# adaLN vectors made on TensorE, and native fp32 for the first sixteen products of both up products, in a diffusion block on one core

## The chip, the cores and the metric

The kernel runs on one core of one Trainium2 chip. The metric is the device time of one execution in microseconds. A core has TensorE (matrix products into PSUM), VectorE, ScalarE, GpSimd, and queues that issue DMAs; here SyncE's queue (SP) issues almost all loads and stores.

## The reference

A block of a diffusion model: 1024 latent tokens `x` of width 1024, 256 context tokens `ctx`, two conditioning vectors `c` (for the latent tokens) and `c_ctx` (for the context).

```python
def adaln(cond, w, b):                      # w: 1024 x 9216
    m = jax.nn.silu(cond) @ w + b
    return [t[..., None, :] for t in jnp.split(m, N_MOD, axis=-1)]   # nine vectors of 1024

def half_step_ffn(x, mods, g_pre, g_post, w_gu, w_down):
    shift, scale, gate = mods
    h = modulate(rms_norm(x, g_pre), shift, scale)
    g, u = jnp.split(h @ w_gu, 2, axis=-1)                           # the up product, 2 x 2816 wide
    y = (jax.nn.silu(g) * u) @ w_down                                # the down product
    return x + 0.5 * gate * rms_norm(y, g_post)
```

Vectors 0, 1 and 2 are shift, scale and gate of the first FFN, 3, 4 and 5 those of the middle part (a gated short convolution beside an S5 scan, joined by an output projection), 6, 7 and 8 those of the second FFN. Latent and context tokens go through the first FFN and into the S5 scan; behind it only the latent tokens go on. All inputs are fp32.

## The kernel before

**Products and operands.** A product of two fp32 matrices is made from operands that are split in two parts of the type fp32r: ScalarE copies the high part, VectorE subtracts it from the source (`split`, line 157; `wop` for weights, 591; `hop` for activations, 494). Three fp32r products then stand for one: high x high, high x low, low x high.

**The latent up product** (`g_lat`, 596) is a Strassen-like scheme: for each of 22 column blocks `f` of 128 gate and 128 up columns there are seven products `m` = 1 to 7 instead of eight, each over four k-tiles of 128 and 512 columns, so 4 x 3 matmuls of 128x512. 22 x 7 = 154 products form one FFN. `seq` is their order by hand: first sixteen early ones (`order1`, `order2`: m = 1 for f = 0 to 3, then m = 2, 5 and 3 likewise), then the rest. `prep` (656) forms the weight operand of one product from raw weight tiles (for m = 1 and 2 a half of one tile, for m = 5 a sum, for m = 3 three operations), with sums on VectorE, and splits it; `prod` (687) issues the matmuls and the evacuation from PSUM; `prepare` (756) runs `prep` up to four products ahead. Raw weights stand in four tiles `wr` of 512 KB; `fetch` (646) may load a tile anew when the last product that needs the old content has been prepared (`loads[...][2] < done`). `hops` (499) forms the seven activation operands in the order m = 1, 2, 5, 3, 7, 6, 4, the later ones in place over the earlier (`self.sub(b11, b12, b11)` for m = 5), and keeps the split ones in `hb`.

**The start.** `run` (1629) loads four blocks of `x`, then the columns of vectors 1 and 0 of adaLN in two halves of 512 columns, then four more blocks of `x`. Strings written by hand give the order in which the pieces are issued: `S0` loads, `S1` the hops (`h`), the normalization of the second blocks (`q`), the second half of adaLN (`a`), weight fetches (`f`), preparations (`w`) and products (`p`, `P`). VectorE keeps the order of the program in this part (`G0`); elsewhere a planner orders the instructions of each engine.

**adaLN before.** For each row tile of 128 of `w_ada`, VectorE multiplies a 128x1024 tile by the column of silu(c) in `scol` and adds to an accumulator (`ada_acc`, 280); eight tiles give one vector for one condition. `ada_col` (287) turns the accumulator by a 32x32 transpose and a reduction on VectorE and one small product on TensorE. For vectors 0 and 1 of the latent tokens the sum over partitions is made by `first_sum` (380) with a column of ones.

**Fillers.** Work that may lie anywhere in a stage is a generator, and `self.step()` (122) advances it: in the first FFN after 34 empty steps (`FW`) vectors 1 and 0 for the context, then 2, 3 and 4 for both conditions, then `s5_params` (1088), three steps (`FN`) at each product with m = 3, 4 or 6, so nine per seven products; before the last products the filler is run to its end and the normalization of the context follows (`side`, 1761). In the down stage vectors 5 and 6 are the filler (`fill56`, 1798), in the S5 stage vector 7 (1860), in the second FFN vector 8 (`fill3`, 2011). `ada_mods` (332) loads each 512 KB tile of `w_ada` two steps ahead into a ring of five tiles `tb`, which the early products also use for their results.

**Lines in the profile.** All instructions are issued through one helper, `Lane.call`, so nearly all rows have line 51; rows are told apart by their tiles: `z` large operands and hops, `w` split weights, `wr` raw weights, `t` temporaries, `tb` the ring, `scol` silu of the conditions, `ps` PSUM, `red` and `mod` the adaLN columns, `sd` the stored result of the up product.

Of the kernel before, what the change touches and what calls it, by code (L numbers as in the profile page):

```python
# [13 lines left out]
OP = mybir.AluOpType  # L14
AX = mybir.AxisListType

P = 128
# [51 lines left out]
class Kernel:  # L69
# [111 lines left out]
    def setup(self):  # L181
# [41 lines left out]
        nc.vector.tensor_copy(self.scol, pt[:, :16])  # L223
        self.ones = self.t(cp, [P, 1], "ones")
# [130 lines left out]

    def first_loads(self, side):

        self.mt = self.t(self.cp, [P, 2, KT], "mt")
        for mod in range(2):
            self.modc[mod, 0] = self.mt[:, mod, :]  # L360
# [26 lines left out]
    def first_cols(self, half, pt):  # L387
        sl = slice(4 * half, 4 * half + 4)
        b2 = self.cols[:, 0:16].rearrange("p (m k) -> p m k", m=2)
        self.add(self.mt[:, :, sl], pt[:, :8].rearrange("p (m k) -> p m k", m=2), b2[:, :, sl])  # L390
        self.stt(self.mt[:, 1, sl], self.mt[:, 1, sl], 1.0, self.gpre(0)[:, sl], OP.add, OP.mult)
# [107 lines left out]
    def hops(self, stages, blocks, hb):  # L499
# [4 lines left out]
        for src, m in stages:  # L504
# [8 lines left out]
            for k in range(4):  # L513
# [82 lines left out]
    def g_lat(self, wgu, hb, sd, fills, early, late, held):  # L596
# [59 lines left out]
        def prep(f, m):  # L656
# [26 lines left out]
            wops[f, m] = self.wop(x)  # L683
# [3 lines left out]
        def prod(f, m):  # L687
# [7 lines left out]
            for k in range(4):  # L695
                wh, wl = w[:, 0, k * P : (k + 1) * P], w[:, 1, k * P : (k + 1) * P]
# [57 lines left out]
        look, done = 4, 0  # L754

        def prepare(n, eager=True):
            nonlocal done
            while done < min(n, len(seq)):
                fetch(done)
                prep(*seq[done])  # L760
# [4 lines left out]
        def step(n):  # L765
            prod(*seq[n])

# [12 lines left out]
        for n in range(next(count), len(seq)):  # L780
# [4 lines left out]
            if seq[n][1] in (3, 4, 6):  # L785
                self.step(fills)
# [1320 lines left out]
```

## Time and profile before

| what | value |
|---|---|
| median of 3 runs | 2108.68 us (2104.74 to 2113.64) |
| the profiled execution's own time | 2107.51 us |
| its span (first to last instruction) | 2105.7 us |
| TensorE, busy time | 1937.8 us, 9018 matmuls |
| VectorE, busy time | 1586.3 us, 2727 instructions |
| ScalarE, busy time | 838.5 us, 1482 instructions |
| GpSimd, busy time | 199.7 us, 106 instructions |
| DMA | 368.30 MB, mean 175 GB/s |

Times in the profile run from the span's start. Busy is the time in which an engine has an instruction under way; matmuls are pipelined, so a busy TensorE is not always at its peak. The clock column is TensorE's granted clock as a share of full speed, the DMA column the busy share of the core's 16 DMA engines. The stages in order: start and up product of the first FFN to about 556, up product of the context to about 723, the down products to about 1000, the projections, S5 and convolution to about 1250, output projection to about 1403, second FFN's up product to about 1885, its down product to the end.

### The profile page before, as it was taken

How to read it: one execution, taken by the hardware profiler on the slowest of the kernel's cores; microseconds unless marked ns; L12 is line 12 of the kernel's file. 1: busy time of each engine (PE TensorE's matmuls, PEld its weight loads, DVE VectorE, ACT ScalarE, POOL GpSimd, SP SyncE). 2: the span in 40 equal slices, each digit the busy share in tenths (PEclk: the TensorE clock that was granted, in tenths of full speed). 3: DMA queues.
4: the chain of work that ended last, by engine and by line, in shares of the span. 5: the costliest groups of instructions: out<-in, count | busy, mean ns of one | idle time of the engine just before them, and what ended most of it. 6: DMA issues, size and time to landing. Idle time of an engine off the chain costs nothing.

```text
span 2105.7 us, 25356 instructions
## 1 busy us (share of the span) xinstructions
PE 1937.8 (92%) x9018; PEld 1592.4 (76%) x9018; DVE 1586.3 (75%) x2727; ACT 838.5 (40%) x1482; POOL 199.7 (9%) x106
## 2 busy tenths in 40 slices
PE   5879989898898979999999899997999999999997
PEld 4568876686798867877887787775788888887775
DVE  6689998998865678798637986488865555576977
ACT  5433323243343334466532334354333333334543
POOL 0000000042336200000002430010000000000000
PEclk9889999999999989999999999998999999999999
DMA  8347453255578989367587543143642222277554
GB/s 299 93 146 253 141 177 113 86 146 169 170 224 240 343 303 303 117 239 257 173 234 222 189 141 110 40 151 97 202 150 80 84 86 81 84 252 267 192 189 152
DMA packets 342604, 368.30 MB, mean 175 GB/s; under 512 B 47376, under 2 KB 254924, under 8 KB 342476
## 3 DMA queue, kind: packets, MB, share of 16 engines
q1 hardware_dynamic: 340172, 358.28, 53.3%
q10 hardware_dynamic: 2304, 8.39, 1.0%
q8 instruction: 71, 1.16, 0.2%
q14 instruction: 57, 0.47, 0.1%
HBM read 294.50 MB, written 74.17 MB: 175 GB/s over the span
## 4 chain that ended last, share of the span: by engine, by line
PE 61%; DVE 21%; DMA 9%; issue 4%; ACT 2%; POOL 1%; SPq 1%; DVEq 0%; ACTq 0%; POOLq 0%
PE ps L51 61%; DVE t L51 7%; DVE z L51 6%; DVE w L51 4%; DVE tb L51 3%; DMA wr<-in_ffn_w_gu 2%; DMA tb<-in_w_ada 2%; DMA wr<-in_ffn_w_down 1%; SPq L51 1%; POOL tb L51 1%; DMA z<-in_w_ada 1%; ACT w L51 1%; DMA z<-sd 1%; ACT t L51 1%; ACT z L51 1%
## 5 line engine op out<-in xcount | busy, mean ns | idle before, releaser
L51 PE MATMUL ps<-z,w 128*128 128x512 f32 (+1 forms) x5712 | 1262.3, 382 | 83.1 <-ACT w L51 38.2
L51 PEld LDWEIGHTS ps<-z,w 128*128 128x128 f32 x5712 | 1019.7, 194 | 304.4 <-ACT w L51 44.8
L51 PE MATMUL ps<-w,w 128*128 128x512 f32 x1848 | 434.5, 396 | 19.5 <-DVE w L51 14.1
L51 PEld LDWEIGHTS ps<-w,w 128*128 128x128 f32 x1848 | 350.3, 191 | 101.2 <-DVE w L51 20.2
L51 ACT ACTIVATE w<-wr 128x512 fp32r<-128x512 f32 (+1 forms) x286 | 215.8, 758 | 360.1 <-PE ps L51 280.2
L51 DVE TENSOR_TENSOR w<-wr,w 128x512 fp32r<-128x512 f32 (+1 forms) x280 | 253.4, 909 | 94.4 <-ACT w L51 88.5
L51 ACT ACTIVATE w<-t 128x512 fp32r<-128x512 f32 x308 | 186.9, 626 | 270.5 <-DVE t L51 181.8
L51 DVE TENSOR_TENSOR w<-t,w 128x512 fp32r<-128x512 f32 x308 | 212.8, 701 | 61.5 <-ACT w L51 61.2
L51 DVE TENSOR_TENSOR t<-t,ps 128x512 f32<-128x512 f32 x150 | 102.5, 685 | 66.5 <-PE ps L51 65.7
L51 ACT ACTIVATE w<-z 128x512 fp32r<-128x512 f32 x110 | 69.2, 630 | 148.3 <-PE ps L51 142.2
L51 DVE TENSOR_TENSOR t<-wr 128x512 f32<-128x512 f32 x148 | 101.1, 695 | 30.9 <-DMA wr<-in_ffn_w_down 15.0
L51 ACT ACTIVATE t<-ps 128x512 f32<-128x512 f32 (+2 forms) x135 | 73.7, 548 | 118.3 <-PE ps L51 116.8
L51 DVE TENSOR_TENSOR z<-z,z 128x512 fp32r<-128x512 f32 (+3 forms) x127 | 102.1, 839 | 13.9 <-DMA z<-z 7.1
L51 DVE SCALAR_TENSOR_TENSOR tb<-tb,scol 128x1024 f32<-128x1024 f32 x77 | 98.1, 1283 | 6.9 <-DMA tb<-in_w_ada 6.7
L51 DVE TENSOR_TENSOR w<-z,w 128x512 fp32r<-128x512 f32 x110 | 76.0, 691 | 30.2 <-ACT w L51 30.0
L51 ACT ACTIVATE t<-z 128x1024 bf16<-128x1024 f32 (+3 forms) x132 | 75.4, 605 | 44.7 <-DVE z L51 31.4
L51 ACT ACTIVATE t<-t 128x512 f32<-128x512 f32 (+1 forms) x83 | 51.9, 625 | 103.2 <-DVE t L51 102.7
L51 POOL TENSOR_TENSOR z<-z,z 128x1024 f32<-128x1024 f32 x24 | 84.7, 3552 | 80.0 <-PE ps L51 44.3
L51 PE MATMUL ps<-z,t 128*128 128x512 f32 x384 | 89.9, 395 | 1.1 <-ACT t L51 1.1
L51 PEld LDWEIGHTS ps<-z,t 128*128 128x128 f32 x384 | 72.1, 188 | 18.4 <-ACT t L51 1.5
L51 POOL TENSOR_TENSOR tb<-tb 128x512 f32<-128x512 f32 x24 | 35.8, 1506 | 456.1 <-DVE t L51 434.9
L51 DVE TENSOR_TENSOR z<-t,ps 128x512 f32<-128x512 f32 (+1 forms) x52 | 29.6, 570 | 53.3 <-PE ps L51 52.6
(124 smaller groups left out, 1391.0 us busy)
## 6 DMA issues: line engine op xcount, KB each, us to landing
wr<-in_ffn_w_gu SPq DMA_DIRECT2D x156, 512.0 KB, 4.4
wr<-in_ffn_w_down SPq DMA_DIRECT2D x198, 256.0 KB, 4.5
tb<-in_w_ada SPq DMA_DIRECT2D x64, 512.0 KB, 4.5
sd<-z SPq DMA_DIRECT2D x44, 512.0 KB, 4.7
z<-sd SPq DMA_DIRECT2D x88, 256.0 KB, 5.4
z<-in_w_ada SPq DMA_DIRECT2D x24, 512.0 KB, 6.0
wr<-in_ffn_w_down SPq DMA_DIRECT2D x22, 512.0 KB, 4.5
wr<-in_w_in SPq DMA_DIRECT2D x20, 512.0 KB, 4.6
```

Source lines behind the costliest of these rows:

```text
L51: r = f(*a, **kw)
```

## The change

adaLN is computed on TensorE for all vectors but 8. `srep` holds each column of silu(c) and silu(c_ctx) alternately 32 columns wide; with it as the 128x32 stationary operand, a product with 256 columns of `w_ada` gives both conditions at once in 32 partitions of PSUM, and four such products go to the four groups of 32 partitions (columns of the array). All operands are plain fp32. For vectors 0 and 1 this stands at the start (`first_mm`), for both conditions. Vectors 2 to 7 are one filler of the first FFN (`ada_pe`): four loads in the first four of seven steps, then sixteen products in one burst, two bursts a vector, then a copy, two transposes and two additions. The fillers of the down stage and the S5 stage fall away. TensorE keeps the program's order in the start and in the whole up product of the first FFN. The filler advances twelve steps per seven products, after 22 empty ones.

In both up products the sixteen early products take plain fp32 operands: the weight operand isn't split, and `hr` keeps the unsplit activation. A raw weight tile used by the early products with m = 1 or 2 is loaded anew only when those products have been issued (`free`). The split activations are still made, for the other 18 blocks.

```diff
 def setup
+        self.srep = self.t(cp, [P, KT, 32], "srep")
+        nc.scalar.activation(
+            self.srep.rearrange("p k (n c) -> p n c k", c=2),
+            pt[:, :16].rearrange("p (c k) -> p c k", c=2).unsqueeze(1).to_broadcast([P, 16, 2, KT]), AF.Copy,
+        )
...
+    def ada_pe(self, plan, gap):
+        nc = self.nc
+        seq = [(n, b) for n in range(len(plan)) for b in range(2)]
+        after = iter(())
+
+        def cols(pt, mod, done):
+            rows = self.t2([P, 256])
+            nc.scalar.activation(rows, pt[:, :256], AF.Copy)
+            yield
+            pt = self.ps()
+            for b in range(2):
+                self.tr(pt[:, b * P : b * P + P], rows[:, b * P : b * P + P], P)
+            for cond in range(2):
...
+                col = self.t(self.cp, [P, KT], f"mod{mod}_{cond}")
+                self.add(
+                    col.rearrange("p (j b) -> p j b", b=2),
+                    pt[:, : 2 * P].rearrange("p (b j r) -> p j b r", b=2, j=4)[:, :, :, cond],
+                    self.b_ada(mod).rearrange("p (j b) -> p j b", b=2),
+                )
+                self.modc[mod, cond] = col
+            yield
+            if done:
+                yield from done() or ()
+
+        for n, b in seq:
+            ws = []
+            for g in range(gap):
+                if g < 4:
+                    ws.append(self.ada_load(plan[n][0], 4 * b + g, self.ta()))
+                next(after, None)
+                yield
+            if b == 0:
+                pt = self.ps()
+            for k, w in enumerate(ws):
+                for j in range(4):
+                    nc.tensor.matmul(
+                        pt[32 * j : 32 * j + 32, :256], self.srep[:, 4 * b + k, :], w[:, 256 * j : 256 * j + 256],
+                        start=b == 0 and k == 0, stop=b == 1 and k == 3,
+                    )
+            self.td_(*ws)
...
-    def first_acc(self, mod, acc):
-        for kt in range(KT):
-            self.ada_acc(acc, self.ws[mod, kt // 2][:, kt % 2, :], kt, 0)
-            yield
-
-    def first_sum(self, mod, acc, pt):
-        for k in range(4):
-            c = 4 * mod + k
+    def first_mm(self, pt, mod, kt, w):
+
+        for h in range(2):
+            j = 32 * (2 * mod + h)
             self.nc.tensor.matmul(
-                pt[:, c : c + 1], acc[:, k * P : (k + 1) * P], self.ones, start=True, stop=True
+                pt[j : j + 32, :256], self.srep[:, kt, :], w[:, 256 * h : 256 * h + 256], start=kt == 0, stop=kt == KT - 1
             )
...
 def hops
+                if m in hr:
+                    hr[m].append(c)
...
 def g_lat
+        nraw = sum(m in (1, 2) for _, m in early)
+
+        def free():
+            return min(done, sent) if sent < nraw else done
 
         def fetch(n, most=len(loads)):
-            while most and at[0] < len(loads) and (n is None or loads[at[0]][3] <= n) and loads[at[0]][2] < done:
+            while most and at[0] < len(loads) and (n is None or loads[at[0]][3] <= n) and loads[at[0]][2] < free():
...
-            wops[f, m] = self.wop(x)
+            wops[f, m] = x if (f, m) in early else self.wop(x)
...
             for k in range(4):
+                if (f, m) in early:
+                    nc.tensor.matmul(pt, w[:, k * P : (k + 1) * P], hr[m][k], start=first and k == 0, stop=k == 3, **on)
+                    continue
...
-            if seq[n][1] in (3, 4, 6):
-                self.step(fills)
+            self.step(fills[seq[n][1] - 1])
             step(n)
...
 def run
+        for mod in (1, 0):
+            for kt in range(KT):
+                self.first_mm(pt, mod, kt, self.ws[mod, kt // 2][:, kt % 2, :])
+        self.scale(xt, self.rsq(ss), nc.scalar)
...
 def accs2
             for kt in range(KT):
-                self.ada_acc(acc, self.ws[kt], kt, 0)
-                yield
-            for mod in range(2):
-                self.first_sum(mod, acc[:, mod, :], pt)
+                for mod in range(2):
+                    self.first_mm(pt, mod, kt, self.ws[kt][:, mod, :])
...
 def fill
-            yield from self.ada_mods([
-                (1, (1,), lambda: self.ada_scale(1, 1, 0)),
-                (0, (1,), None),
-                (2, (1, 0), gates1),
-                (3, (1, 0), None),
-                (4, (1, 0), scales4),
-            ])
+            yield from self.ada_pe([
+                (2, gates1),
+                (3, None),
+                (4, scales4),
+                (5, lambda: self.ada_gate(5, 0, 1, False, 2)),
+                (6, None),
+                (7, lambda: self.ada_scale(7, 0, 2)),
+            ], GAP)
             yield from self.s5_params()
...
+        self.nc.order(True, "tensor")
         for _ in ffn:
             pass
+        self.nc.order(False, "tensor")
...
-        def fill56():
-            for _ in range(DW):
-                yield
-            yield from self.ada_mods([
-                (5, (0,), lambda: self.ada_gate(5, 0, 1, False, 2)),
-                (6, (0,), None),
-            ])
-
-        self.fill = fill56()
...
-        self.fill = self.ada_mods([(7, (0,), lambda: self.ada_scale(7, 0, 2))], 1)
...
-S1 = 'wahhaahaahafPpaaqwhafpahpwhwhhwqqqqqqqqqqqqpqqqqPeePhhhPhhhhehPhhpewwhhhPPPphPwhhehPh'
+S1 = 'whhhhfPpaqwhafphpwhwhhwqqqqqqqqqqqqpqqqqPeePhhhPhhhhehPhhpewwhhhPPPphPwhhehPh'
...
-DW = 0
-FW = 34
-FN = 3
+FW = 22
+FN = (2, 2, 1, 1, 2, 2, 2)
+GAP = 7
...
-G0 = ('vector',)
+G0 = ('vector', 'tensor')
```

## Rows read from the trace of the kernel before

**Rows 1.** The page's first part: busy us (share of the span) xinstructions.
```profile
PE 1937.8 (92%) x9018; PEld 1592.4 (76%) x9018; DVE 1586.3 (75%) x2727; ACT 838.5 (40%) x1482; POOL 199.7 (9%) x106
```

**Rows 2.** Windows: stretch, length, busy us by engine, clock, DMA share, GB/s.
```profile
28.00:116.80 88.80, 66.07 (x256) 49.58 (x256) 62.44 (x101) 42.09 (x71) 0.00 (x0) 0.85 0.44 138
116.80:356.70 239.90, 226.69 (x942) 180.37 (x942) 223.19 (x334) 78.36 (x136) 0.00 (x0) 0.96 0.56 175
356.70:500.00 143.30, 134.07 (x564) 106.98 (x564) 126.53 (x315) 48.54 (x83) 35.76 (x24) 0.98 0.41 117
500.00:556.00 56.00, 52.31 (x255) 42.55 (x254) 47.14 (x83) 25.14 (x45) 2.89 (x3) 0.97 0.63 200
723.00:768.00 45.00, 34.04 (x140) 26.15 (x138) 44.69 (x66) 16.01 (x28) 0.00 (x0) 0.91 1.04 393
1060.00:1112.00 52.00, 49.70 (x268) 42.26 (x267) 22.32 (x23) 17.84 (x33) 2.73 (x1) 1.00 0.88 223
1403.20:1483.20 80.00, 60.47 (x257) 46.05 (x255) 65.72 (x114) 43.21 (x75) 2.41 (x1) 0.87 0.41 125
1483.20:1885.00 401.80, 400.04 (x1724) 324.47 (x1724) 244.16 (x378) 140.08 (x241) 0.00 (x0) 1.00 0.37 120
```

**Rows 3.** Lines by form, TensorE, windows 2, 3, 4, 4, 5 and 8 above.
```profile
L51 PE MATMUL ps<-z,w 128*128 128x512 f32 x924 | 226.5, 406 | 17.1 <-ACT z L51 9.9 <-ACT w L51 3.2 <-DVE tb L51 2.4
...
L51 PE MATMUL ps<-z,w 128*128 128x512 f32 x561 | 134.3, 400 | 9.2 <-ACT w L51 7.3 <-DVE t L51 1.8
...
L51 PE MATMUL ps<-z,w 128*128 128x512 f32 x174 | 43.9, 408 | 3.1 <-ACT w L51 2.5 <-DVE t L51 0.4 <-ACT t L51 0.2
L51 PE MATMUL ps<-z,w 128*128 128x256 f32 x65 | 8.2, 282 | 0.0
...
L51 PE MATMUL ps<-w,w 128*128 128x512 f32 x132 | 33.4, 410 | 2.6 <-DVE w L51 1.9 <-ACT w L51 0.6
...
L51 PE MATMUL ps<-z,w 128*128 128x512 f32 x1657 | 386.3, 395 | 1.8 <-DVE w L51 1.6 <-ACT w L51 0.2
```

**Rows 4.** Lines by form, VectorE, 116.8 to 356.7: the adaLN groups.
```profile
L51 DVE SCALAR_TENSOR_TENSOR tb<-tb,scol 128x1024 f32<-128x1024 f32 x56 | 71.1, 1283 | 4.6 <-DMA tb<-in_w_ada 4.5
...
L51 DVE STREAM_TRANSPOSE tb<-tb 128x1024 f32<-128x1024 f32 x8 | 10.0, 1245 | 0.0
L51 DVE TENSOR_REDUCE red<-tb 128x32 f32<-128x1024 f32 x8 | 9.7, 1218 | 0.0
```

**Rows 5.** Lines by form, TensorE, whole run: a native fp32 product's instructions.
```profile
L51 PE MATMUL ps<-tb,z 128*128 128x160 f32 x128 | 21.0, 311 | 2.1 <-DMA z<-pd 2.1
```

**Rows 6.** Timeline of TensorE in the S5 stage: start, length, form, count.
```profile
1121.84 2.78 PE L51 MATMUL ps<-tb,z 128*128 128x160 f32 x20
...
1163.47 1.05 PE L51 MATMUL ps<-t,z 128*128 128x128 f32 x8
```

**Rows 7.** Timeline of all engines, 84 to 92: early products with m = 3.
```profile
84.56 0.63 ACT L51 ACTIVATE w<-t 128x512 fp32r<-128x512 f32 x1 [8.56 <-DVE t L51]
85.22 0.69 DVE L51 TENSOR_TENSOR w<-t,w 128x512 fp32r<-128x512 f32 x1 [0.69 <-ACT w L51]
85.24 3.31 PE L51 MATMUL ps<-z,w 128*128 128x512 f32 x12 [2.18 <-ACT w L51]
...
89.85 0.69 DVE L51 TENSOR_TENSOR t<-t,wr 128x512 f32<-128x512 f32 x1 [3.33 <-DMA wr<-in_ffn_w_gu]
...
91.98 5.49 PE L51 MATMUL ps<-z,w 128*128 128x512 f32 x12 [3.42 <-ACT w L51]
```

**Rows 8.** The page's DMA issues: KB each, us to landing.
```profile
wr<-in_ffn_w_gu SPq DMA_DIRECT2D x156, 512.0 KB, 4.4
```

**Rows 9.** Waits from 723 to 768: us in total, times, longest.
```profile
ACT w L51 <- DMA wr<-in_ffn_w_down: 18.7, 9, 4.2
...
PE ps L51 <- DVE red L51: 8.4, 1, 8.4
```

**Rows 10.** Lines by form, VectorE, 1060 to 1112: vector 7.
```profile
L51 DVE SCALAR_TENSOR_TENSOR z<-z,scol,z 128x1024 f32<-128x1024 f32 x7 | 11.1, 1589 | 14.3 <-DMA z<-in_w_ada 14.3
```

More of the change, by code (lines that the diff above doesn't have):

```diff
@@ L354, in ada_mods @@
                 yield
+    def ada_pe(self, plan, gap):
[10 more added lines that the diff above has]
+            for cond in range(2):
+                if (mod, cond) in self.modc:
+                    continue
[25 more added lines that the diff above has]
+            self.td_(*ws)
+            if b == 1:
+                for _ in after:
+                    pass
+                after = cols(pt, *plan[n])
+        yield from after
     def first_loads(self, side):
-        self.mt = self.t(self.cp, [P, 2, KT], "mt")
+        self.mts = [self.t(self.cp, [P, 2, KT], f"mt{cond}") for cond in range(2)]
         for mod in range(2):
-            self.modc[mod, 0] = self.mt[:, mod, :]
+            for cond in range(2):
+                self.modc[mod, cond] = self.mts[cond][:, mod, :]
         self.ws = {}
@@ L373, in first_loads @@
             yield
[L375 to L382 removed]
+    def first_mm(self, pt, mod, kt, w):
+        for h in range(2):
+            j = 32 * (2 * mod + h)
             self.nc.tensor.matmul(
[L384 removed]
+                pt[j : j + 32, :256], self.srep[:, kt, :], w[:, 256 * h : 256 * h + 256], start=kt == 0, stop=kt == KT - 1
             )
     def first_cols(self, half, pt):
[L388 to L391 removed]
+        nc = self.nc
+        rows = self.t2([P, 256])
+        nc.scalar.activation(rows, pt[:, :256], AF.Copy)
+        pt = self.ps()
+        for b in range(2):
+            self.tr(pt[:, b * P : b * P + P], rows[:, b * P : b * P + P], P)
+        sl = slice(4 * half, 4 * half + 4)
+        b2 = self.cols[:, 0:16].rearrange("p (m k) -> p m k", m=2)[:, :, sl].rearrange("p m (h b) -> p m h b", b=2)
+        rt = pt[:, :256].rearrange("p (b m h r) -> p m h b r", b=2, m=2, h=2)
+        for cond in range(2):
+            m = self.mts[cond][:, :, sl]
+            self.add(m.rearrange("p m (h b) -> p m h b", b=2), rt[:, :, :, :, cond], b2)
+            self.stt(m[:, 1], m[:, 1], 1.0, self.gpre(0)[:, sl], OP.add, OP.mult)
     def rsq(self, ss):
@@ L497, in hop, with hops @@
         return o
-    def hops(self, stages, blocks, hb):
+    def hops(self, stages, blocks, hb, hr):
         t = [[], []]
@@ L594, in wop, with g_lat @@
         return o
-    def g_lat(self, wgu, hb, sd, fills, early, late, held):
+    def g_lat(self, wgu, hb, hr, sd, fills, early, late, held):
         nc = self.nc
@@ L759, in prepare @@
                 fetch(done)
+                if any((seq[done][0], side) not in raws for side in A[seq[done][1]]):
+                    break
                 prep(*seq[done])
@@ L765, in step @@
         def step(n):
+            nonlocal sent
             prod(*seq[n])
+            sent = n + 1
+            if n < nraw:
+                fetch(None)
         count = itertools.count()
@@ L1641, in run @@
         hb = {m: [] for m in range(1, 8)}
+        hr = {m: [] for m in (1, 2, 5, 3)}
         xt = [self.z() for _ in range(4)]
@@ L1726, in run @@
         hs = [k for k, c in enumerate(S1) if c == "h"]
-        assert S1[: hs[5]].count("a") == 10 and S1[: hs[9]].count("q") == 17
+        assert S1[: hs[5]].count("a") == 2 and S1[: hs[9]].count("q") == 17
         act.update(h=lambda: next(h), q=lambda: next(q), a=lambda: next(a))
@@ L1936, in run @@
         hb = {m: [] for m in range(1, 8)}
+        hr = {m: [] for m in (1, 2, 5, 3)}
         def spl(g):
```

32 lines of the change are left out of this document (7 added, 25 removed).

## The prediction

> **What bounds it now.** The page's first part comes first: TensorE is busy for 92% of the span [rows 1]. A share over the whole run doesn't say where time is lost, so next the windows, cut where the work changes [rows 2], and beside them the count of matmuls in each stretch [rows 3]. The latent up product of the second FFN (1483 to 1885) is the yardstick: 1657 matmuls of 128x512 cover 386.3 us, 0.233 us each, TensorE never waits and the clock is granted in full. Holding the other stretches against 0.233 us shows what each loses. The first FFN from 116.8 to 356.7: 924 x 0.233 = 215.4 us and 3 us of small products, of 239.9: 21 lost. VectorE is busy for 223 of those 240 us; its largest group is the adaLN accumulation, 56 operations of 1283 ns, and with 8 transposes and 8 reductions adaLN takes 91 us of it [rows 4]. From 356.7 to 500 (the S5 parameters): 561 x 0.233 = 130.8 of 143.3, 12 lost. From 500 to 556: 174 x 0.233 + 65 half-width ones at 0.126 + 2 = 50.8 of 56, 5 lost. The start of each up product loses most in proportion: 28 to 116.8 holds the sixteen early products, 192 x 0.233 = 44.8 us of products in 88.8; 1403 to 1483 holds the same in 80. The start of the down stage, 723 to 768, is bounded otherwise: 132 x 0.233 = 30.8 in 45 us, with DMA at 1.04 of its engines and VectorE busy for 44.7. The reader is to see: TensorE sets the time, and what is lost sits where VectorE or DMA is full.
>
> **The change, part by part.** *adaLN leaves VectorE in the first FFN.* Gone are 91 us of VectorE work between 116.8 and 356.7. What it costs now is only the 21 us that TensorE loses there; I take 19 back, bounds 8 and 21, since evacuations and operand splits stay on VectorE (132 us over 240) and can delay a product at times.
>
> *adaLN arrives on TensorE.* Six vectors (2 to 7) x 8 row tiles x 4 products = 192 native fp32 products, each with a 128x32 stationary and 256 columns. In the trace a native product is two instructions: the S5 stage's 64 products of 160 columns are 128 of them, of 311 ns each [rows 5], and twenty of them take 2.78 us [rows 6], so they follow each other by (2.78 - 0.31)/19 = 130 ns; for 128 columns it is about (1.05 - 0.3)/7 = 107 ns. That is 0.83 ns a column in each instruction. So 256 columns cost 2 x 213 = 427 ns, and all of them one behind the other 192 x 0.427 = 82 us: the upper bound. All of it lies on the path, for TensorE has no gap there that lasts. The four products of a row tile go to four different quarters of the array's columns. If four run beside each other, the bound below is 82/4 = 20.5 us. The two instructions of one product share a quarter; if starts keep the program's order, only the second of one and the first of the next run together, which gives 41 us. No row of before shows products on part of the columns, so I take 29 us, between four at once and pairs, and keep 20.5 and 82 for the range. The twelve bursts' edges, the transposes that turn the rows into columns (12 of 128x128 at 0.1) and their copies: +3 us, bounds 1 and 8.
>
> The Trainium skill, "TensorE: Matmul & The Clock Gate", section "Measured speedup vs the span model", gives 2.38x for three column tiles; the same share of four would make the 82 us an estimated 26. Against the change speaks "TensorEngine Tiling (Array Packing)", section "Key Properties": changing the tiling mode drains the engine, so 12 bursts drain it 24 times; the page has no price, and no run here shows one.
>
> *The S5 parameters follow.* Their filling steps come 12 per seven products instead of 9, so the same VectorE work falls on fewer products. Nothing taken off the 17 us lost between 356.7 and 556; bounds 12 lost more and 12 gained. A burst on TensorE also lets VectorE catch up.
>
> *The two vectors at the outset.* Eight accumulations of full and sixteen of half width leave VectorE; both conditions are now made at once, which also drops sixteen loads of 512 KB later. In their place TensorE gets 32 native products per half in program order. Two early products precede those of the second half and the rest stand behind them, so TensorE waits there until the last w_ada tile lands. I count nothing for this alone, nor for the one copy on ScalarE that spreads the conditioning columns: their cover is the DMA of the start, for which before waits too; without it the second half's 32 products are 14 us serial, inside the bounds that follow.
>
> *Native fp32 for sixteen products.* Removed per product: a ScalarE copy of 0.63 us, a VectorE subtraction of 0.69 and the hand-overs between them, 16 times in each FFN; TensorE's start on them is the pattern in [rows 7], where sum, copy and matmul follow each other and then VectorE waits 3.33 us for the next weight tile. Added: a product is 4 x 2 x 0.427 = 3.41 us instead of 12 x 0.233 = 2.80, +0.62, or +10 us of TensorE work per FFN, in stretches that hold 44.8 us of products in 88.8 and 80. And a weight tile is freed only when its product has run, not when it was split: the loads of the next weights (4.4 us to land, [rows 8]) start up to three products later for the second four. From 82 us on, each early product still waits for a load and three VectorE operations, 6.7 us a product as before [rows 7], less the split (1.3 us). A new wait: the subtractions that form the later operands overwrite tiles that native products still read, and splits and evacuations queue behind them on VectorE; the products concerned stand a whole group of four earlier, which is the cover. First FFN: four products' splits and the VectorE time freed, -8, bounds -14 and +5. Second FFN: -5, bounds -12 and +8. If the cover were gone, each would be +10.
>
> *Vectors 5 and 6 leave the down stage, 7 the S5 stage.* From 723 to 768 this takes away up to 16 loads (8.4 MB, 21 us at the window's 393 GB/s), 18 us of VectorE accumulation and the single largest wait, 8.4 us of TensorE for the reduction of vector 6 [rows 9]. What remains late there is the 512-column weight loads, on which ScalarE waited 18.7 us, now with a freer queue. TensorE needs 32 of the 45 us: -11, bounds -13 and -4. In 1060 to 1112 TensorE is nearly full (49.7 of 52), though VectorE stood 14.3 us for w_ada [rows 10]; the loads that end there delay what follows: -3, bounds -8 and 0. SP's queue loses these 40 loads (24 of them move ahead to the first FFN, where DMA is at 0.56 and sixteen others vanish).
>
> Sum against the profiled execution's own 2107.5 us: -19 + 29 + 3 + 0 - 8 - 5 - 11 - 3 = -14, so 2093.5. The median of the three runs lies 1.2 us above that execution, hence 2095.
>
> **Rivals.** *The column tiles run one behind another* (ends on the other side): each burst of 16 products takes 6.8 us, 82 in all, 53 more than taken: 2148. For it: every native row of before is serial, and an instruction that must wait for its own quarter holds up those behind it. Against: consecutive products write different quarters. It decides from 43 us, or 224 ns a product; below, the change gains. *Pairs only, and denser S5 steps:* 41 us, and 6 us more lost from 356 to 500: 2113, no change. For it: VectorE is already busy for 127 of 143 us there. *Native products bind at the start of both FFNs:* +10 each in place of -8 and -5 would be 2128 in full, 2111 where half of it shows. Against: 30 us lost in each. *VectorE's release reaches further:* the S5 stretch and the tail lose nothing more either, 17 us less: 2078. For it: with adaLN gone VectorE has slack ahead of these steps.
>
> **How the numbers follow.** The sum's own case has 0.46, from 2082 to 2107; serial tiles 0.21; pairs with denser S5 steps 0.16; native products binding 0.05; the further release 0.12. A measurement tells 0.5% (10.5 us) of this kernel from no change: faster means under 2098, slower over 2119. Of the first case 0.40 is faster and 0.06 about the same. Faster: 0.40 + 0.12 = 0.52; same: 0.06 + 0.16 + 0.05 = 0.27; slower 0.21. The range 2070 to 2140 takes in the release and the sum's bounds, but of the serial case only the part in which other bounds give 8 us or more back: it leaves out some 0.04 below and 0.15 above.
>
> **What would show it.** In the trace after: bursts of 32 instructions of 256 columns; a burst of 1.7 us means four at once, 3.4 pairs, 6.8 serial. The stretch of the first FFN behind its sixteen early products should lose under 10 us besides the bursts; VectorE is no longer busy for nine tenths of it. Early products show 3.4 us each; the sixteenth should end before 107 us. The down stage's first 132 matmuls should take 32 to 36 us with no wait for a reduction. The prediction is wrong if bursts are serial, if TensorE waits for w_ada inside a burst, or if the early products wait longer for weights than before.

## The result and the profile after

The changed kernel takes 2086.68 us (median of 4 runs, 2085.83 to 2087.14) beside 2108.51 for the kernel before in the same session: the ratio is 0.9898, interval 0.9886 to 0.9911. That is 1.0% or 21.8 us faster. The profiled execution's span is 2084.7 us, 21.0 below that of before, and the places below account for these 21.0.

The page's first part, after:
```profile
PE 1964.9 (94%) x9364; PEld 1565.0 (75%) x9364; DVE 1428.5 (69%) x2532; ACT 824.0 (40%) x1459; POOL 199.2 (10%) x106
```
TensorE has more work than before and VectorE 158 us less [rows 1]. Next the windows, cut where the work changes as in [rows 2] (stretch, length, busy us of TensorE, its weight loads, VectorE, ScalarE, GpSimd, then clock, DMA share, GB/s):
```profile
28.00:110.20 82.20, 65.58 (x237) 30.87 (x236) 43.94 (x79) 31.75 (x55) 0.00 (x0) 0.93 0.45 146
110.20:319.90 209.70, 206.94 (x1155) 156.03 (x1155) 115.07 (x205) 67.72 (x119) 0.00 (x0) 0.98 0.60 204
319.90:468.00 148.10, 136.57 (x556) 107.78 (x555) 136.54 (x327) 50.52 (x86) 33.85 (x24) 0.95 0.43 125
468.00:562.00 94.00, 93.91 (x458) 78.36 (x459) 61.33 (x99) 39.22 (x69) 6.54 (x4) 1.00 0.48 150
723.00:768.00 45.00, 45.00 (x209) 37.58 (x209) 35.34 (x57) 21.13 (x38) 0.00 (x0) 1.00 0.85 288
1386.50:1464.50 78.00, 66.19 (x193) 31.91 (x191) 57.32 (x100) 35.30 (x62) 2.36 (x1) 0.93 0.43 135
1464.50:1866.00 401.50, 399.20 (x1717) 322.94 (x1718) 244.99 (x379) 140.62 (x242) 0.00 (x0) 1.00 0.37 118
```
The lines by form of TensorE for the second to fourth of these windows:
```profile
L51 PE MATMUL ps<-z,w 128*128 128x512 f32 x756 | 184.5, 403 | 8.6 <-ACT z L51 7.9 <-DVE z L51 0.7
L51 PE MATMUL ps<-tb,srep 128*32 128x256 f32 x384 | 23.2, 382 | 0.0
L51 PE MATMUL ps<-ident,t 128*128 128x128 f32 x12 | 2.5, 291 | 2.0 <-ACT t L51 2.0
L51 PE MATMUL ps<-ident,mod 128*8 128x128 f32 x3 | 0.8, 272 | 0.0
...
L51 PE MATMUL ps<-z,w 128*128 128x512 f32 x553 | 136.6, 409 | 11.1 <-DVE t L51 8.1 <-ACT t L51 3.0
...
L51 PE MATMUL ps<-z,w 128*128 128x512 f32 x348 | 82.5, 396 | 0.5 <-DVE t L51 0.5
L51 PE MATMUL ps<-z,w 128*128 128x256 f32 x94 | 11.6, 283 | 0.0
```
And TensorE's timeline (start, length, form, count, wait before): two early stretches, the first two bursts, and the start of the down stage:
```profile
95.23 7.10 PE L51 MATMUL ps<-z,t 128*128 128x512 f32 x16 [1.36 <-DVE t L51]
110.26 3.66 PE L51 MATMUL ps<-z,w 128*128 128x512 f32 x7 [7.92 <-ACT z L51]
...
160.21 1.93 PE L51 MATMUL ps<-tb,srep 128*32 128x256 f32 x32
162.07 14.26 PE L51 MATMUL ps<-z,w 128*128 128x512 f32 x60
176.26 1.93 PE L51 MATMUL ps<-tb,srep 128*32 128x256 f32 x32
...
725.10 60.05 PE L51 MATMUL ps<-w,w 128*128 128x512 f32 x264
```
The reader is to see four things. First, a burst of sixteen products delays the next product's start by 162.07 - 160.21 = 1.86 us; twelve are 22.3. Second, in the bursts' stretch 756 x 0.233 + 22.3 + 3.3 of small products are 201.8 of 209.7: 8 lost, where before 21 were [rows 2, 3]. Of the waits in these lines the 7.92 us for ScalarE's operand lie ahead of the window's first matmul; inside it TensorE waits 0.7 us for VectorE once and 2.0 for the rows' copies, and most of the rest of the 8 is lost at its start: after the 7.92 us in which TensorE stood, the granted clock is 0.76 of full speed in the mean of the first 20 us, a mix of its two levels (1.2 and 2.4 GHz). The window of it alone:
```profile
110.20:130.00 19.80, 19.06 (x63) 14.31 (x64) 19.76 (x37) 9.58 (x18) 0.00 (x0) 0.76 0.41 120
```
63 matmuls, 14.7 us at 0.233, take 19.8 there. Third, the S5 parameters lose more, 148.1 - 553 x 0.233 = 19 where it was 12, but the stretch behind them nothing more, where it was 5. And last, the down stage runs 264 matmuls in one piece.

Where the 21.0 us came from, by the start of each stage in the two traces:

| stage: what ends it | ends at, before | after | gain |
|---|---|---|---|
| early products: first product behind them | 116.81 | 110.26 | 6.5 |
| rest of the first FFN's up products: first down matmul | 723.12 | 725.10 | -8.5 |
| down stage: first matmul of the projections | 1033.06 | 1017.57 | 17.5 |
| projections: first S5 product | 1121.84 | 1105.14 | 1.2 |
| S5 stage: second FFN's first transposition | 1403.24 | 1386.53 | 0 |
| its early products: first product behind them | 1483.42 | 1464.53 | 2.2 |
| to the end | 2105.7 | 2084.7 | 2.1 |

So the first FFN gained nothing as a whole: what adaLN gave back to TensorE there was less than what it took. The gain is the down stage's.

### The profile page after: what moved, and what is told of

The parts are those of the page before. It is cut to its first block, busy times and chain, and to the rows that moved or that the text cites. A ratio compares the mean times of both kernels' runs of the same rounds, so it can differ in the third digit from the quotient of the medians.

```text
span 2084.7 us, 25831 instructions
## 1 busy us (share of the span) xinstructions
PE 1964.9 (94%) x9364; PEld 1565.0 (75%) x9364; DVE 1428.5 (69%) x2532; ACT 824.0 (40%) x1459; POOL 199.2 (10%) x106
## 4 chain that ended last, share of the span: by engine, by line
PE 55%; DVE 14%; DMA 4%; issue 2%; ACT 2%; POOL 1%; SPq 0%; DVEq 0%; ACTq 0%; POOLq 0%
PE ps L51 55%; DVE z L51 5%; DVE t L51 5%; DVE w L51 2%; DMA wr<-in_ffn_w_down 2%; DMA wr<-in_ffn_w_gu 1%; ACT t L51 1%; ACT w L51 1%; DVE sy L51 0%; POOL t L51 0%; DMA z<-scd 0%; ACT z L51 0%; DMA pd<-z 0%; DMA pd<-tb 0%; DVE sq L51 0%
## 5 line engine op out<-in xcount | busy, mean ns | idle before, releaser
L51 PE MATMUL ps<-z,w 128*128 128x512 f32 (+1 forms) x5328 | 1151.2, 377 | 40.9 <-DVE w L51 15.1
L51 PEld LDWEIGHTS ps<-z,w 128*128 128x128 f32 x5328 | 938.5, 192 | 236.2 <-DVE w L51 17.4
L51 PE MATMUL ps<-w,w 128*128 128x512 f32 x1848 | 427.3, 392 | 14.8 <-DVE w L51 8.6
L51 ACT ACTIVATE w<-wr 128x512 fp32r<-128x512 f32 (+1 forms) x270 | 206.5, 766 | 342.0 <-PE ps L51 278.9
L51 DVE TENSOR_TENSOR w<-wr,w 128x512 fp32r<-128x512 f32 (+1 forms) x264 | 243.5, 924 | 135.9 <-ACT w L51 129.6
L51 ACT ACTIVATE w<-t 128x512 fp32r<-128x512 f32 x292 | 177.0, 626 | 220.8 <-DVE t L51 132.2
L51 DVE TENSOR_TENSOR w<-t,w 128x512 fp32r<-128x512 f32 x292 | 198.5, 692 | 89.9 <-ACT w L51 89.7
L51 PE MATMUL ps<-z,t 128*128 128x512 f32 x512 | 151.4, 456 | 18.0 <-DVE t L51 11.8
L51 PEld LDWEIGHTS ps<-z,t 128*128 128x128 f32 x512 | 97.9, 193 | 69.8 <-issue 40.4
L51 ACT ACTIVATE z<-z 128x512 fp32r<-128x512 f32 (+2 forms) x76 | 48.3, 673 | 63.7 <-DVE z L51 63.7
```

The costliest lines, as they stand in the source:

```text
L51: r = f(*a, **kw)
```

## The experiments

Ratios are to the kernel before on the same chip; the change's own is 0.9898, so 0.01 of ratio more is 21 us slower than the change.

**One part alone.** First adaLN on TensorE without the native products: every early weight operand is split again.
```diff
-        nraw = sum(m in (1, 2) for _, m in early)
+        nraw = 0
...
-            wops[f, m] = x if (f, m) in early else self.wop(x)
+            wops[f, m] = self.wop(x)
...
-                if (f, m) in early:
-                    nc.tensor.matmul(pt, w[:, k * P : (k + 1) * P], hr[m][k], start=first and k == 0, stop=k == 3, **on)
-                    continue
```

> The changed kernel without native products: the sixteen early products of both FFNs are split as before, adaLN stays on TensorE. My theory: adaLN carries most of the gain (the down stage's 17 us), native products give about 2 us in the second FFN and 3 to 4 in the first, so this comes to some 2092 us, with the second FFN's sixteen early products back at about 80 us instead of 78 and the first FFN's later start of the rest. Rival: the earlier start in the first FFN (110.3 instead of 116.8 us) comes from VectorE's release by adaLN alone and native products are worth nothing there: 2089. Second rival: native products bind at both starts, and without them it is faster than the changed kernel: under 2085.

2093.6 us, ratio 0.9937 (0.9924 to 0.9950): some 8 us short of the whole change. The profiled execution has 5.8 of them: the first product behind the early ones starts at 111.26 (1.0 later), two more waits of 0.64 and 1.01 follow it, the down stage starts 3.3 later in all, and the second FFN's early products take 80.4 us, not 78.0. Then the native products alone, added to the kernel before: the same lines the other way round, with `hr`, `sent`, `free` and the order of the loads as in the change.
```diff
...
-            wops[f, m] = self.wop(x)
+            wops[f, m] = x if (f, m) in early else self.wop(x)
...
```

> The kernel before with native fp32 for the sixteen early products of both FFNs, adaLN on VectorE as before. My theory: 2 us gained in the second FFN and 2 to 4 in the first, 2103 us. Rival: with the accumulations still on VectorE the early products of the first FFN wait for VectorE anyway, so only the second FFN's 2 us show: 2106. Second rival: TensorE's 10 us more per FFN are on the path: 2115 or more.

2111.92 us, ratio 1.0019 (1.0008 to 1.0030): nothing gained. My theory said 2103 and missed. In its trace the early products of the second FFN do gain 3.0 us, but those of the first FFN none (117.25 beside 116.81), and the S5 stage is 4.7 us longer, for which I have no cause. That stage lasts 281.4 us before and after, but 5.0 and 3.4 more also in the two other runs of the kernel before below, whose edits lie in the first FFN; so these 4.7 can't be put down to native products. By the times the two parts are not a sum: 13 us gained by the one and 4 lost by the other make 9, and together they gain 21. By the traces, native products let the first FFN go on 1.0 us earlier where adaLN is on TensorE and 0.4 later where it is not; that VectorE's load makes this difference is argued, not shown.

**The price of a burst.** The loops of a burst exchanged, so that each quarter's four products follow one another:
```diff
-            for k, w in enumerate(ws):
-                for j in range(4):
+            for j in range(4):
+                for k, w in enumerate(ws):
```

> The changed kernel with the two loops of a burst exchanged: the four row tiles of one column quarter follow each other, then the next quarter; the same 16 products. If an instruction that waits for its own quarter holds up those behind it, the eight instructions of a quarter run one after the other and a burst takes about 6.4 us instead of 1.9, twelve bursts 55 us more: about 2140. If TensorE hands instructions to the quarters ahead of those that wait, a burst stays near 1.9 us and the time at 2087. In between (3 to 4 us a burst) would mean that only a few instructions are looked ahead.

2119.75 us, ratio 1.0061 (1.0046 to 1.0075): 33 us slower than the change. TensorE's timeline of it:
```profile
160.89 4.59 PE L51 MATMUL ps<-tb,srep 128*32 128x256 f32 x32
165.42 14.21 PE L51 MATMUL ps<-z,w 128*128 128x512 f32 x60
```
A burst now takes 4.53 us, 2.67 more, and 12 x 2.67 = 32 us is nearly all that the run lost: the bursts lie on the path in full. The order decides, as expected, but 4.53 is neither the serial 6.8 nor free. So a third order, two quarters in turn:
```diff
-            for k, w in enumerate(ws):
-                for j in range(4):
+            for k, w, j in [(k, w, h + j) for h in (0, 2) for k, w in enumerate(ws) for j in range(2)]:
+                if True:
```

> The change, with each burst's products ordered over two quarters at a time (quarters 0 and 1 in turn through the four tiles, then 2 and 3); the same products, nothing left out. With four quarters in turn a burst took 1.86 us, quarter by quarter 4.53. If a product waits only for the one before it in its own quarter, two run at once: 3.4 us a burst, 18 us more over the twelve, 2105. If what counts is that no two neighbours in the queue go to one quarter, the burst stays near 1.9 to 2.2 us and the time at 2087 to 2091. If four at once came from another reason (a switch of quarter itself costs), the burst lies at 4 us or more: 2113 or above.

2095.0 us, ratio 0.9947 (0.9927 to 0.9967), and on TensorE's timeline:
```profile
159.33 2.82 PE L51 MATMUL ps<-tb,srep 128*32 128x256 f32 x32
162.09 14.22 PE L51 MATMUL ps<-z,w 128*128 128x512 f32 x60
```
2.76 us a burst, so 12 x 0.90 = 10.8 more than the change, and the ratio says 10. None of the three numbers I had written down was met. Call a round the products that follow each other in different quarters. With one quarter a round is one product and takes 4.53 / 16 = 0.283 us, with two in turn 2.76 / 8 = 0.345 for two, with four 1.86 / 4 = 0.465 for four: a fixed 0.22 for each round and 0.06 for each product in it fits all three. Why a round costs that is not settled.

**The S5 parameters, denser.** An empty step after every second of their steps, so that eight work per seven products and not twelve:
```diff
-            yield from self.s5_params()
+            for k, _ in enumerate(self.s5_params()):
+                yield
+                if k % 2:
+                    yield
```

> The changed kernel with an empty filling step after every second step of the S5 parameters, so that they come 8 per seven products instead of 12. My theory: the 18.8 us lost between 320 and 468 come from VectorE being full there (137 of 148 us) while the next 94 us lose nothing with VectorE at 61 of 94; spread out, half of it is given back: 5 to 10 us gained, 2078 to 2082. Rival: the losses come from chains within the S5 parameters that delay an operand whatever their density: 2087, no change. Second rival: the end of the filler now collides with the context's normalization and the early preparation for the next stage: 2 to 5 us slower.

2078.23 us, ratio 0.9857 (0.9838 to 0.9876): some 8 us faster than the change, and the down stage starts 10.4 earlier. Its windows over the S5 parameters and behind them:
```profile
319.60:468.00 148.40, 142.77 (x606) 114.15 (x605) 136.53 (x327) 55.11 (x93) 34.01 (x24) 0.98 0.41 119
468.00:514.00 46.00, 44.87 (x195) 35.98 (x194) 33.63 (x63) 17.65 (x32) 0.00 (x0) 1.00 0.58 178
```
606 matmuls where the change has 556 in as long a stretch. TensorE's one long wait left there, 5.2 us for VectorE, ends at 436.7. It follows a piece of GpSimd's work, on the timeline of VectorE and GpSimd:
```profile
423.55 3.97 POOL L51 TENSOR_TENSOR tb<-tb 128x512 f32<-128x512 f32 x3 [5.92 <-DMA pd<-tb]
423.76 0.68 DVE L51 TENSOR_TENSOR t<-t,ps 128x512 f32<-128x512 f32 x1
425.14 1.23 DVE L51 TENSOR_TENSOR z<-t,t 128x512 f32<-128x512 f32 x1 [0.70 <-ACT t L51]
426.29 1.77 DVE L51 TENSOR_TENSOR t<-wr 128x512 f32<-128x512 f32 x1
428.25 4.24 POOL L51 TENSOR_TENSOR tb<-tb 128x512 f32<-128x512 f32 x3 [0.73 <-DMA pd<-tb]
431.28 1.75 DVE L51 TENSOR_TENSOR t<-t,wr 128x512 f32<-128x512 f32 x1
```
Operations of 0.69 us take 1.2 to 1.8 there, but the one at 423.76, which reads PSUM beside one tile, keeps its 0.68. So the next run spreads twice (six steps per seven products) and moves GpSimd's complex products to VectorE:
```diff
-            self.cmul(er, ei, x0, x1, v0, v1, xt, pl if b % 2 else None)
+            self.cmul(er, ei, x0, x1, v0, v1, xt)
...
-            yield from self.s5_params()
+            for _ in self.s5_params():
+                yield
+                yield
```

> The changed kernel with the S5 parameters spread further than in the run with an empty step after every second (here one after each, 6 steps per seven products), and the complex products that GpSimd made moved to VectorE (24 operations of 128x512, 17 us). In that run VectorE's 128x512 operations of 0.69 us took 1.2 to 1.8 us where GpSimd worked, and TensorE lost 10 us there. If this contention is what is left, the stretch from 320 to 530 loses under 5 us: 2070 to 2074. If VectorE's greater load costs as much as the contention did: 2078 as before. If the filler now runs into the end of the stage and is drained there: slower than 2078.

2077.3 us, ratio 0.9860 (0.9846 to 0.9875): as fast as the one before it, not measurably faster, but the window is now without loss:
```profile
318.00:468.00 150.00, 150.00 (x645) 120.48 (x645) 133.54 (x342) 60.13 (x100) 0.00 (x0) 1.00 0.39 117
```
The run makes two edits at once, so it doesn't tell which of them emptied the window. Both runs are faster than the change and than the kernel before. Is it the spreading by itself? The same edit (nine steps become six) in the kernel before:

> The kernel before with the parameters of the S5 blocks spread as in the run of the change with an empty step after every second one (nine steps per seven products become six that work). Nothing is left out. If spreading them pays by itself, because each step lets VectorE's operand work run late beside GpSimd (12 us lost before in 356.7 to 500, 5 in 500 to 556), this run gains 8 to 12 us: about 2097. Rival: the room for spreading comes from the change, which moves the parameters forward by some 37 us; from their old place they then run into the down products' start or the queue's drain at its end, where TensorE stands still: 2105 to 2125.

2118.13 us, ratio 1.0033 (1.0017 to 1.0048): slower. Its windows, cut at 460, 500 and 556:
```profile
356.70:460.00 103.30, 100.24 (x423) 80.31 (x423) 88.97 (x271) 41.26 (x69) 5.58 (x3) 0.98 0.35 100
460.00:500.00 40.00, 39.30 (x170) 31.53 (x168) 34.65 (x43) 10.96 (x19) 22.52 (x18) 1.00 0.50 146
500.00:556.00 56.00, 44.48 (x199) 35.25 (x200) 45.16 (x80) 21.30 (x40) 8.64 (x8) 0.88 0.65 189
```
By 500 it has gained 593 - 564 = 29 matmuls [rows 2], some 7 us; from 500 to 556 it holds 199 where before has 255, for the rest of the parameters lands there. The first down matmul comes 4.0 us later than before; the other 6 us of the profile's 10.3 lie behind it, 3.4 of them in the S5 stage, and have no shown cause. The change starts the parameters 37 us earlier, which is the room in which spreading pays there.

**The down stage.** Two runs put back what vectors 5 and 6 had done there, the loads alone and the VectorE work alone (nothing reads either):
```diff
+        def fill56():
+            for mod in (5, 6):
+                for kt in range(KT):
+                    w = self.ada_load(mod, kt, self.ta())
+                    self.td_(w)
+                    yield
+
+        self.fill = fill56()
```

> The changed kernel with the sixteen 512 KB loads of vectors 5 and 6 put back into the down stage as its filler, with nothing computed from them (they are in the trace only as DMA). If DMA pressure made the old loss of 14 us at the start of this stage, the first 132 matmuls take 40 to 45 us again and the whole run is 10 to 14 us longer: about 2098. If VectorE and the wait for the reduction made it, the loads are hidden: 2087 to 2089.

2105.01 us, ratio 0.9991 (0.9981 to 1.0000): the run is 19 us longer than the change, where I had expected 10 to 14. Fourteen of the sixteen loads are issued between 715 and 753 us. The window at the start of the stage:
```profile
725.00:770.00 45.00, 37.58 (x159) 28.89 (x158) 28.41 (x44) 16.06 (x29) 0.00 (x0) 1.00 1.04 410
```
from the waits of the same window (us in total, times, longest):
```profile
ACT w L51 <- DMA wr<-in_ffn_w_down: 21.6, 9, 4.5
```
and from TensorE's timeline the first matmul of the down stage and the first of the projections:
```profile
724.47 16.49 PE L51 MATMUL ps<-w,w 128*128 128x512 f32 x72
...
1031.26 33.71 PE L51 MATMUL ps<-z,w 128*128 128x512 f32 x144
```
DMA is at 1.04 again, as in [rows 2], and ScalarE waits for weights for 21.6 us (18.7 in [rows 9]); after the change this wait is not among the stage's at all. The down stage lasts 306.8 us, beside 292.5 after the change and 309.9 before: the loads alone put back 14.3 of the 17.5 us. In the nine traces of this case without these loads the stage lasts 291.4 to 293.1 us, and 309.1 to 310.3 in the four with loads and arithmetic, so the 3 us that are left are more than the spread. Whether they are VectorE's or the wait for the reduction, no run shows. Some 5 us more of this run's loss stand behind the down stage, 1.9 in the S5 stage and 3.4 behind the second FFN's early products, where nothing was put back.

The VectorE work without the loads, in the same place:
```diff
...
+                for kt in range(KT):
+                    self.ada_acc(acc, w, kt, 0)
+                    yield
+                nc.vector.transpose(w, acc)
...
```

> The changed kernel with the VectorE work of vectors 5 and 6 put back into the down stage (16 operations of 128x1024, two transposes, two reductions, 25 us, on tiles that are already there), without the loads and without TensorE's small products behind it; the results are used for nothing. If VectorE made the old loss, 8 to 12 us longer: about 2097. If DMA made it, or the wait of TensorE for the reduction, which this kernel leaves out: 2087 to 2090.

2091.73 us, ratio 0.9935 (0.9911 to 0.9958), a profiled span of 2085.1. This run missed its target: its accumulations depend on no load, and in the trace they stand between 440 and 520 us, not in the down stage. So it says nothing on VectorE's share there, and no run shows what the arithmetic would cost without the loads.

**VectorE's release.** 64 accumulations of 128x1024 put back beside the bursts (nothing reads them):
```diff
+        idle = self.z()
+        fresh = [True]
...
+            for k, w in enumerate(ws):
+                for cond in range(2 if n < 2 else 1):
+                    self.ada_acc(idle, w, 0 if fresh[0] else 4 * b + k or 1, cond)
+                    fresh[0] = False
             self.td_(*ws)
```

> The changed kernel, which still makes adaLN on TensorE, with 64 accumulations of 128x1024 (82 us of VectorE) on the same tiles put back beside the bursts in the first FFN; their results are used for nothing. If releasing VectorE is what took the loss between 116.8 and 356.7 from 21 to 9 us, the stretch of the bursts loses some 12 us more and the run takes about 2099. If the loss was not VectorE's, the time stays at 2087 to 2090. More than 2105 would mean that VectorE was the larger part of what the bursts pay for.

2087.99 us, ratio 0.9907 (0.9888 to 0.9926): no loss. Its window of the stretch, with VectorE at 88% where the change has 55%:
```profile
108.80:319.00 210.20, 207.14 (x1155) 155.76 (x1155) 185.65 (x269) 68.58 (x118) 0.00 (x0) 0.98 0.61 204
```
My theory (2099) fell. A second candidate was one wait of before: TensorE stood 6.0 us for its own small product of a gate at 270 us, and few products ran around it:
```profile
270.35 0.37 PE L51 MATMUL ps<-ident,mod 128*8 128x128 f32 x1 [6.00 <-DVE mod L51]
```
In the kernel before, that product was put off:
```diff
-        yield
+        for _ in range(4):
+            yield
         pt = self.ps()
...
-FW = 34
+FW = 28
```

> The kernel before with one edit: the transposition of a gate's column is issued four filler steps after VectorE's product for it instead of one, and the side queue starts six steps earlier, so that what comes behind stands about where it stood. Nothing is left out. The theory left after the run that kept VectorE busy: a part of what the kernel before lost between 116.8 and 356.7 us was TensorE's own small product standing in its queue for VectorE (6.0 us of waiting at 270 us, and in 260 to 280 us 54 products where 88 ran in the slices on either side: 34 x 0.233 = 8 us). By it this run is some 8 us faster than before, 2098, and 260 to 280 us hold 85 to 88 products. Rival: VectorE is late there whatever asks for it, so the loss only moves to the next weight operand that it is late with: 2104 to 2108, and TensorE's waits in the stretch sum to what they did.

2112.32 us, ratio 1.0018 (1.0005 to 1.0030): nothing gained, as the rival said, though its 2104 to 2108 was missed too. The wait is gone and 260 to 280 us are full, but others stand in the slice before it, where VectorE is busy for 19.8 of 20 us, and TensorE's waits in the stretch, without that for its first operand, sum to 11 us where they were 13. The windows:
```profile
240.00:260.00 20.00, 18.13 (x78) 13.82 (x77) 19.82 (x34) 3.97 (x7) 0.00 (x0) 1.00 0.45 138
260.00:280.00 20.00, 20.00 (x88) 15.99 (x88) 19.97 (x27) 6.79 (x13) 0.00 (x0) 1.00 0.65 211
```
TensorE's timeline:
```profile
243.08 3.07 PE L51 MATMUL ps<-z,w 128*128 128x512 f32 x12 [0.69 <-ACT t L51]
247.06 3.59 PE L51 MATMUL ps<-z,w 128*128 128x512 f32 x14 [0.91 <-ACT w L51]
```
The profiled span is even 2.2 us longer. The question was then why 82 us more of VectorE's work had cost nothing beside the bursts. This run doubles the accumulations of two more vectors: 80 in place of 64.
```diff
-                for cond in range(2 if n < 2 else 1):
+                for cond in range(2 if n < 4 else 1):
```

> The change, with 80 accumulations of 128 x 1024 beside the bursts instead of the 64 of the run that kept VectorE busy (some 102 us of VectorE's work, nothing read from it): its stretch then holds about 206 us of VectorE's work in 210, 98%, where that run stood at 88% and the kernel before at 93%. The theory now: VectorE's release is worth something, but only from the point where VectorE is full; what put 82 us back without loss was that TensorE's bursts (22 us) give VectorE time to catch up. By it the waits come back here: the stretch grows by 8 to 20 us and the run stands 8 to 20 us above that one, 2096 to 2108. Rival: VectorE's occupancy doesn't matter there at all, and the loss of before lay in something else that the change took away: 2085 to 2091.

2106.42 us, ratio 0.9994 (0.9981 to 1.0008): 20 us more of VectorE's work cost 18 us, where the first 82 cost none. Its window:
```profile
110.00:320.00 210.00, 197.91 (x1068) 147.84 (x1069) 195.58 (x265) 64.85 (x111) 0.00 (x0) 0.94 0.63 200
```
from TensorE's lines by form its products in it:
```profile
L51 PE MATMUL ps<-z,w 128*128 128x512 f32 x703 | 175.7, 411 | 8.6 <-ACT z L51 7.9 <-DVE z L51 0.7
L51 PE MATMUL ps<-tb,srep 128*32 128x256 f32 x352 | 23.0, 394 | 8.6 <-DMA tb<-in_w_ada 8.6
```
and from the timeline of all engines the burst that waits longest:
```profile
280.02 1.50 PE L51 MATMUL ps<-tb,srep 128*32 128x256 f32 x24
...
280.73 1.28 DVE L51 SCALAR_TENSOR_TENSOR z<-tb,scol,z 128x1024 f32<-128x1024 f32 x1
...
282.07 0.33 SPq L51 DMA_DIRECT2D tb<-in_w_ada  x1
...
286.05 1.08 PE L51 MATMUL ps<-tb,srep 128*32 128x256 f32 x8 [4.53 <-DMA tb<-in_w_ada]
```
VectorE is at 93%, the share of before, and a loss is back, but not the one of before. The products with split operands wait for VectorE for 0.7 us, as in the change. It is the bursts that wait, 8.6 us, for tiles of `w_ada` that are loaded late: the last load ahead of this wait is issued at 282.07, as one of the added accumulations ends (280.73 + 1.28), and the burst goes on at 286.05. And the 48 matmuls behind each of the two longest waits take 13.5 and 13.3 us where 11.4 are usual, at a granted clock of 0.82 and 0.85 in the mean. So this run shows a price of holding the ring, which the added work itself made; it doesn't show that a full VectorE is what the kernel before lost by. Of the 13 us that the change gained in this stretch the cause stays open. A rival that no run tests is the order: the change keeps TensorE in program order in this stage, where the kernel before left it to the planner.

## Why the prediction was right, and where its steps were not

The forecast, 2095 and faster, held, and the range with it. That it missed by no more owes something to luck: the bursts cost 7 us less and the down stage gave 6 more than taken, while VectorE's release gave 6 less. The yardstick holds, though TensorE does wait in that stretch, for 1.8 us [rows 3]. By its own terms, against the profiled execution's sum of -14 (measured: -21):

- **Bursts, 29 taken: 22.3.** The bursts come out near the bound below (20.5), not between it and pairs. The serial rival is excluded, but the run that goes quarter by quarter shows what it hung on: there 0.283 us a product is already past the 224 ns from which it was to decide. The rule of the Trainium skill in "TensorE: Matmul & The Clock Gate", section "Measured speedup vs the span model", 2.38x for three column tiles, had made an estimated 26; four in turn measure 82 / 22.3 = 3.7x against the serial estimate, but 4.53 / 1.86 = 2.4x against the same products quarter by quarter, so it depends on what one calls serial.
- **VectorE's release in the first FFN, -19 taken: -13** (21 lost, then 8, of which the copies and the clock at its start are most). The size is within its bounds of 8 and 21, but the mechanism is not shown: 82 of the 91 us of VectorE's work, put back into the changed kernel, cost nothing, and 20 more cost time by way of the bursts' tiles and not of the operands.
- **Edges and transpositions, +3: 0.** 3.3 us of small products stand in place of 3.1, and their 2.0 us of waits are in the 8.
- **S5 parameters, 0 taken: +2**, made of +7 where they run and -5 behind them. Spread, they are worth 8 to 10. The further release (2078) was the rival that spoke of this loss; the run that reached its time needed a wider spacing as well.
- **Native products, -8 and -5 taken: -6.5 and -2.2** at these places. The first includes adaLN's release at the outset: without native products 5.5 of the 6.5 remain. So the step that failed here is the term of the two vectors at the outset, put at nothing because the cover was thought to be DMA; it is worth 5.5, and native products in the first FFN's start 1.0 where 8 were taken. Over the whole run native products give some 8 us of time added last (5.8 in the profile) and nothing added first, so a term for each part alone was not enough.
- **Vectors 5 and 6 out of the down stage, -11 taken, bounds -13 and -4: -17.5.** Beyond its bound. The bound took only the first 132 matmuls down to 32 us; they take 30, and the loss of before reached beyond them. I had named three causes, the loads, VectorE and the reduction; the loads alone are 14.3, and the other 3 were not taken apart.
- **Vector 7, -3 taken: -1.2.** Within its bounds. The 2.1 us of the tail and some 3 us in the first FFN belong to no term.

Of what was to show it: the burst of about 1.7 us, VectorE at 55% instead of nine tenths, early products of 3.45 us (eight of the second FFN, 64 instructions, in 27.6) and a sixteenth that ends at 102.3, before 107, all came; the first 132 down matmuls took 30 us, better than 32 to 36.

## What to carry to other kernels

Moving work to the busiest engine can pay if it leaves a stage where a third resource is full: here sixteen loads were most of the price (14 of 17 us), whatever they fed, and a run that puts back the loads alone shows it. An engine that is busy for nine tenths of a stretch need not be what the stretch loses by: put its work back, in one dose and in two, and where time is lost then, read in the trace which wait came back before calling it the old one. Two parts of a change need not add up: run each alone before giving each its term, and when filler work moves forward, look again at how densely it is spaced.

## What the runs showed of the hardware

Native fp32 products with 32 stationary columns take least time if neighbours in the queue go to different quarters of the columns: 1.86 us for sixteen with four quarters in turn, 2.76 with two, 4.53 with one.

VectorE's fp32 operations on two SBUF tiles are slowed beside GpSimd's: the 128x512 product of two temporaries takes 920 ns in the mean in the S5 parameters' window, where GpSimd is busy for 34 us, and 689 from 319.9 to 504 us in the run with GpSimd's products moved, where GpSimd stands idle. The lines by form of VectorE, of the change and of that run:
```profile
L51 DVE TENSOR_TENSOR z<-t,t 128x512 f32<-128x512 f32 x7 | 6.4, 920 | 0.9 <-ACT t L51 0.9
```
```profile
L51 DVE TENSOR_TENSOR z<-t,t 128x512 f32<-128x512 f32 x10 | 6.9, 689 | 1.5 <-ACT t L51 1.4
```
The Trainium skill, "SBUF — State Buffer", section "SBUF: two separate sides", says that a VectorE operation with two SBUF inputs and a GpSimd operation that reads SBUF exclude each other for a whole instruction on the port pair that they share. The timeline of VectorE and GpSimd above agrees as far as it goes: the additions of 0.5 to 1.1 us are no longer than a GpSimd operation there (4.24 us for three), and the operation that reads PSUM beside one tile isn't slowed.
